# Opening phase of a hybrid block: both modulations on TensorE in four column strips, scaling and splitting of the inputs on VectorE

## The chip, the cores and the metric

The kernel runs on one core of one Trainium2 chip. The metric is the device time of one execution in microseconds (us), the median of the runs shown. A profile is one further execution, recorded by the hardware profiler; its span is the part of that execution that the profile covers.

## The reference

One layer of a block with three token mixers. What the change touches stands at its head: two modulation vectors made from `silu(c)` and `silu(c_ctx)`, and the normalised, modulated inputs on which all projections work.

```python
silu_c, silu_cc = jax.nn.silu(c), jax.nn.silu(c_ctx)
sh1, sc1, g1, sh2, sc2, g2 = jnp.split((silu_c @ w_mod + b_mod)[:, None, :], 6, axis=-1)
csh1, csc1, *_ = jnp.split(silu_cc @ w_mod + b_mod, 6)
h = concatenate([rmsnorm(ctx, norm_mix_w) * (1 + csc1) + csh1,      # 256 tokens
                 rmsnorm(x,   norm_mix_w) * (1 + sc1)  + sh1])      # 512 tokens
out = mixer(h)           # combined input projection, three mixers, gates, output projection
x = x + g1 * out
x = x + g2 * swiglu(rmsnorm(x, norm_ffn_w) * (1 + sc2) + sh2)
result = rmsnorm(x, final_norm_w)
```

The model width is 1024, so `w_mod` is 1024 by 6144. The opening phase needs its first 2048 columns (shift and scale), for both vectors.

## The kernel before

Everything is held with channels on the 128 partitions: x is 8 blocks k of 128 channels by 512 tokens, the context 8 blocks by 256. Projections keep 32-bit accuracy by splitting: each input block becomes a rounded high part H (`hlh`) and a rest L (`hll`), each weight likewise, and `dense` (L313) adds three matmuls per block k (H·H, H·L, L·H), 24 for one output tile ("group") of 128 channels by 512 tokens.

Only TensorE follows an order written out by hand (`MANUAL`, L38 and L1680). The other engines and the DMA queue take their instructions in an order that the tile framework makes from the program. All DMAs are issued from SyncE's queue (SP), which issues in its order and waits where a target buffer is still in use.

`startup` (L1416) is the opening phase. It loads x in four pieces, then the items of `LOADS`, then runs through the words of `STEPS`:

- The modulation of block k for vector s (0 latent, 1 context) is made by `modulate` (L421) on VectorE: two multiply-and-sum instructions (L426) over 128x1024 weights `wmod` against `silu_c`, which holds the vector repeated on all partitions (`silu_c`, made by TensorE at L413), then L429 (bias) and L434 (scale). Blocks 6 and 7 of both vectors are made instead on TensorE by `modulate_pe` (L437): `wmodN`, two more 1 MB loads, as moving operand against the silu columns `scol` (L445), turned by transposes (L451).
- `rstd` (L369) makes the reciprocal root mean square on TensorE, ScalarE and VectorE (L378 to L385); L1470 copies its broadcast to `rbs`.
- `scale_in` (L459) makes H and L of a block. Its form "VV" takes VectorE (L465), ScalarE (L466), VectorE (L467). The other forms put the product (L469) or the difference (L472) on GpSimd and take two ScalarE passes (L470, L471). `EL` and `EX` choose the form of each block.
- Weights come by `fetch` (L209): 256 KB pieces, each in three of `W0` slots, split by ScalarE (L216) and by VectorE and GpSimd in turn (L218). Steps `a` and `b` split the pieces of the first three groups, `g` opens a group on one of the gates.
- A digit runs `dense` for that block on all open groups; six groups are open together, and three more run whole (step `G`). `c` and `C` make the context's `rstd`, `h` its scaled blocks `hx`.

So nine groups of 24 matmuls, 216 in all, run in the opening phase. After it, `first` (L1654) begins with projections of the context: the 48 matmuls that read `hx` into a bank. Then the three mixers follow. Step `D` writes the first three gates out (`gate_out`) and gives their weight slots back, `G` the same for its own.

Of the kernel before, what the change touches and what calls it, by code (L numbers as in the profile page):

```python
# [9 lines left out]
F32 = mybir.dt.float32  # L10
# [9 lines left out]
KT = 8  # L20
# [21 lines left out]
KV = 6  # L42
NK = 3
HO = 6
WB = 4
W0 = 28
NG = 3
GATES = [(b, i) for b in range(3) for i in range(4)]
LOADS = "0 s t 1 2 N"
STEPS = "a m b m l 0 P n m w3 w4 wg n 1 m g wg wg g w5 p 2 g m wu 3 4 n wc 6 c m n 5 C 7 S n n D wg wg G G wg h G"  # L50
EL = "VV VG GV GV GV VG GV VG"
EX = "VV VG VV VG VV VG VV VG"
# [87 lines left out]
class Net:  # L140
# [259 lines left out]
    def silu_c(self, c):  # L400


        sp = self.sp
        t = sp.tile([16, 128], F32, name="silu_r")
        self.S.activation(t, c[:, :128], AF.Tanh, scale=0.5)
        self.V.scalar_tensor_tensor(t, t, 1.0, c[:, :128], op0=OP.add, op1=OP.mult)
        out = sp.tile([128, 2, 1024], F32, name="silu_c")

        def part(s, j):
            b = self.acc_bank()  # L410
            for k in range(4):
                r = 8 * s + 4 * j + k
                self.T.matmul(b[:, 128 * k:128 * k + 128], c[:, 128 + r:129 + r].to_broadcast([16, 128]), t,  # L413
                              start=True, stop=True)
            self.S.copy(out[:, s, 512 * j:512 * j + 512], b)
        return out, part

# [3 lines left out]
    def modulate(self, k, s, silu):  # L421

        V, mod, w = self.V, self.mod, self.wm[k]
        for j in range(2):
            junk = self.sp.tile([128, 1024], BF, name="mjunk", bufs=1)
            V.scalar_tensor_tensor(junk, w[:, j], 0.5, silu[:, s], op0=OP.mult, op1=OP.mult,  # L426
                                   accum_out=mod[:, s, 8 * j + k:8 * j + k + 1])
        z = mod[:, s, k:k + 9:8]
        V.tensor_add(z, z, self.bmod[:, k:k + 9:8])  # L429
        self.scales(k, k + 1, (s,))  # L430

    def scales(self, k0, k1, vectors=(0, 1)):
        for s in vectors:
            self.V.scalar_tensor_tensor(self.sv[:, s, k0:k1], self.mod[:, s, 8 + k0:8 + k1], 1.0,  # L434
                                        self.nmw[:, k0:k1], op0=OP.add, op1=OP.mult)

    def modulate_pe(self, sc, ws):  # L437

        S, V, T, sp = self.S, self.V, self.T, self.sp
        n = KT - KV  # L440
        b, bt = self.bank(), self.bank()
        rows = sp.tile([2, 512], F32, name="silu_r")
        for i, w in enumerate(ws):
            for k in range(KT):
                T.matmul(b[:2, 256 * i:256 * i + 256], sc[:, k], w[:, k], start=(k == 0), stop=(k == KT - 1))  # L445
        S.copy(rows[:, :512], b[:2])
        yield
        for i in range(2):
            for j in range(n):
                o = 2 * (n * i + j)  # L450
                T.transpose(bt[:, o:o + 2], rows[:, 256 * i + 128 * j:256 * i + 128 * j + 128], self.ident[:2, :2])  # L451
        for i in range(2):
            V.tensor_add(self.mod[:, :, 8 * i + KV:8 * i + 8].rearrange("p s j -> p j s"),
                         bt[:, 2 * n * i:2 * n * i + 2 * n].rearrange("p (j s) -> p j s", s=2),
                         self.bmod[:, 8 * i + KV:8 * i + 8].unsqueeze(2).to_broadcast([128, n, 2]))
        self.scales(KV, KT)
        yield

    def scale_in(self, x, n, s, k, H, L, rb, eng):  # L459

        S, V, G = self.S, self.V, self.G
        t = self.sp.tile([128, 512], F32, name="nt", bufs=3)[:, :n]
        scale, shift = self.sv[:, s, k:k + 1], self.mod[:, s, k:k + 1]
        if eng == "VV":
            V.scalar_tensor_tensor(t, x, scale, rb, op0=OP.mult, op1=OP.mult)  # L465
            S.activation(H, t, AF.Identity, bias=shift)  # L466
            V.scalar_tensor_tensor(L, t, shift, H.bitcast(F32), op0=OP.add, op1=OP.subtract)  # L467
        else:
            (G if eng[0] == "G" else V).tensor_mul(t, x, rb)  # L469
            S.activation(H, t, AF.Identity, scale=scale, bias=shift)  # L470
            S.activation(t, t, AF.Identity, scale=scale, bias=shift)  # L471
            (G if eng[1] == "G" else V).tensor_sub(L, t, H.bitcast(F32))  # L472
# [943 lines left out]
    def startup(self):  # L1416
# [3 lines left out]
        c = self.col("crows", [16, 144], pool=sp)  # L1420
        self.wm, wn = {}, []
# [4 lines left out]
        def load(z):  # L1426
            if z.isdigit():
                self.wm[int(z)] = sp.tile([128, 2, 1024], F32, name="wmod", bufs=WB)
                self.dma(self.wm[int(z)], a["wmod1"][int(z)])
            elif z == "N":  # L1430
                for i in range(2):
                    w = sp.tile([128, 2, 1024], F32, name="wmod", bufs=WB).rearrange("p a (b c) -> p (a b) c",
                                                                                      c=128 * (KT - KV))
                    self.dma(w, a["wmodN"][i])
                    wn.append(w)
            elif z == "c":
                self.dma(xc, a["ctxT"])
            elif z in "st":
                for key in first:
                    self.fetch(key, False, ["st".index(z)])  # L1440
            elif z == "g":
                self.fetch(next(fetched), False)
            elif z == "u":
                self.aup0 = self.cp.tile([128, 2, 128], F32, name="TC2")
                self.dma(self.aup0, a["aup"][:, :, :128])
                self.aup0 = self.aup(self.aup0)

        for k in range(0, 8, 2):
            self.dma(x[:, k:k + 2], a["xT"][:, k:k + 2])
            if k == 2:  # L1450
                z = self.col("modc", [128, 88], pool=self.kp)
                self.ident = self.col("ident", [128, 128], pool=self.kp)
        self.bmod, self.nmw, self.nfw, self.fnw = (z[:, i:j] for i, j in ((0, 48), (48, 56), (56, 64), (64, 72)))
        cc = z[:, 72:88].rearrange("p (k s) -> p k s", s=2)
# [3 lines left out]
        silu, part = self.silu_c(c)  # L1458
# [6 lines left out]
        for j in range(2):  # L1465
            part(0, j)
        rb = self.bank()
        self.rstd([sq], TL, 1.0 / D, self.bank(), rb)
        rbs = sp.tile([128, 512], F32, name="rbs")
        S.copy(rbs, rb)  # L1470
# [5 lines left out]
        groups, done, had, had_m, had_n, banks = [], [], [], iter(range(KT)), iter(range(KT)), [3]  # L1476
# [7 lines left out]
        def lat(k):  # L1484
            self.scale_in(x[:, k], TL, 0, k, self.hl[0][k], self.hl[1][k], rbs, EL.split()[k])

        active = iter(gates)
        drained = iter([(0, key) for key in gates])
        for z in STEPS.split():
            if z[0] == "w":  # L1490
                load(z[1:])
            elif z.isdigit():
                k = int(z)
                for n, g in enumerate(groups):
                    ks = [j for j in had + [k] if j not in done[n]] if k not in done[n] else []
                    done[n] += ks
                    self.dense(g, ks=ks)
                had.append(k)
            elif z == "m":
                k = next(had_m)  # L1500
                self.modulate(k, 0, silu)
                lat(k)
            elif z == "n":
                self.modulate(next(had_n), 1, silu)
            elif z == "l":
                part(1, 0)
                part(1, 1)
# [24 lines left out]
            elif z == "P":  # L1532
                sc = sp.tile([128, 8, 2], F32, name="scol")
                S.activation(sc, cc, AF.Tanh, scale=0.5)
                V.scalar_tensor_tensor(sc, sc, 1.0, cc, op0=OP.add, op1=OP.mult)
                V.tensor_scalar(sc, sc, 0.5, None, op0=OP.mult)
                pe = self.modulate_pe(sc, wn)
                next(pe)
            elif z == "p":
                next(pe)  # L1540
                for k in range(KV, KT):
                    lat(k)
            elif z == "c":
                sq = sp.tile([128, 512], F32, name="sq0")[:, :TX]
                for k in range(KT):
                    q = sq if k == 0 else sp.tile([128, 512], F32, name="sqt", bufs=3)[:, :TX]
                    S.activation(q, xc[:, k], AF.Square)
                    if k:
                        (G if k % 2 else V).tensor_add(sq, sq, q)
# [7 lines left out]
            elif z == "h":  # L1557
                for k in range(KT):
                    self.scale_in(xc[:, k], TX, 1, k, self.hx[0][k], self.hx[1][k], rcs, EX.split()[k])
# [405 lines left out]
def lay_out(i):  # L1965
# [10 lines left out]
    A["wmod1"] = f(np.stack([A["wmodT"][:8], A["wmodT"][8:16]], 2))  # L1976
    A["crows"] = f(np.concatenate([A["cvec"].reshape(16, 128), np.eye(16, dtype=np.float32)], 1))
    wm = kp(i["w_mod"][0])
    A["wmodN"] = f(np.stack([wm[:, :, 128 * KV:1024], wm[:, :, 1024 + 128 * KV:2048]], 0))
# [59 lines left out]
```

## Time and profile before

| | us |
|---|---|
| median of 3 runs (1488.23 to 1492.89) | 1488.96 |
| the profiled execution | 1493.02 |
| span of its profile | 1491.2 |
| TensorE busy in the span | 1390.2 |
| last record that reads `hx` in the opening (99.16 + 5.83) | 104.99 |

The profile counts time from the start of the span. "Opening" below means the stretch up to 104.99 us. A true 32-bit matmul is recorded as two instructions; the split ones are recorded as one each. In a row of the timeline, "x2" means that two instructions in a row were merged; the time is from the start of the first to the end of the last, and neighbours overlap, so rates are taken from starts.

### The profile page before, as it was taken

What the parts mean: (1) busy time and instruction counts of PE and PEld (TensorE: products, weight loads), DVE (VectorE), ACT (ScalarE), POOL (GpSimd) and SP (SyncE); (2) the same over time, 40 slices, a digit from 0 to 9 for tenths busy, and PEclk for the clock granted to TensorE, in tenths of its full rate; (3) what the DMA queues carried; (4) which work ended last, traced back from release to release, by engine and by line L of the source; (5) the groups of instructions that cost most, each with busy time, mean ns of one, the idle gap of its engine ahead of it and who ended that gap; (6) DMA issues with size and microseconds to landing.
All of it is one profiled execution on the core that took longest, in us unless ns stands there. A gap on an engine that the chain in (4) does not pass through costs nothing. (4 is left out here: it accounts for less than half of the span.)

```text
span 1491.2 us, 21941 instructions
## 1 busy us (share of the span) xinstructions
PE 1390.2 (93%) x8044; PEld 1194.0 (80%) x8044; DVE 962.1 (65%) x1709; ACT 670.4 (45%) x1254; POOL 393.6 (26%) x345
## 2 busy tenths in 40 slices
PE   5898999999979999998998978999998999999997
PEld 3687879887768887786786867877887999998887
DVE  7957662868494576677675856434438988887332
ACT  4456363553234353333463543333336656566231
POOL 4423522424221212312332706124445000000011
PEclk9999999999999999999999989999999999999998
DMA  7533213142453233236446385656622333324331
GB/s 264 194 107 100 95 56 109 51 124 68 121 148 109 76 93 132 89 101 170 151 154 202 113 261 187 188 176 206 202 78 72 121 107 114 108 91 119 98 91 62
DMA packets 99020, 190.37 MB, mean 128 GB/s; under 512 B 10752, under 2 KB 19472, under 8 KB 97760
## 3 DMA queue, kind: packets, MB, share of 16 engines
q1 hardware_dynamic: 98912, 188.97, 40.8%
q8 instruction: 63, 1.03, 0.3%
q14 instruction: 45, 0.37, 0.1%
HBM read 167.27 MB, written 21.14 MB: 126 GB/s over the span
## 5 line engine op out<-in xcount | busy, mean ns | idle before, releaser
L319 PE MATMUL acc<-hlh,w 128*128 128x512 f32 (+1 forms) x1160 | 388.6, 404 | 6.1 <-ACT w L216 2.0
L216 ACT CAST w<-w 128x512 fp32r<-128x512 f32 (+1 forms) x302 | 182.7, 612 | 377.6 <-DMA w<-in_w_main_dram 172.4
L218 POOL TENSOR_TENSOR w<-w,w 128x512 fp32r<-128x512 f32 x125 | 176.8, 1415 | 541.3 <-ACT w L216 482.4
L218 DVE TENSOR_TENSOR w<-w,w 128x512 fp32r<-128x512 f32 x177 | 136.5, 775 | 210.0 <-ACT w L216 166.5
L319 PEld LDWEIGHTS acc<-hlh,w 128*128 128x128 f32 x1160 | 223.0, 192 | 60.1 <-ACT w L216 2.5
L319 PE MATMUL acc<-hll,w 128*128 128x512 f32 (+1 forms) x576 | 229.4, 398 | 3.7 <-DVE hll L472 1.5
L319 PEld LDWEIGHTS acc<-hll,w 128*128 128x128 f32 x576 | 111.0, 193 | 28.5 <-DVE hll L472 1.9
L319 PE MATMUL acc<-t,w 128*128 128x512 f32 x440 | 115.9, 413 | 7.6 <-ACT t L363 2.9
L319 PEld LDWEIGHTS acc<-t,w 128*128 128x128 f32 x440 | 86.1, 197 | 31.2 <-DVE t L364 4.6
L1809 ACT CAST w<-w 128x512 fp32r<-128x512 f32 x140 | 85.1, 623 | 33.4 <-PE bank L1852 25.7
L1810 DVE TENSOR_TENSOR w<-w,w 128x512 fp32r<-128x512 f32 x140 | 94.9, 688 | 5.0 <-ACT w L1809 4.6
L358 PE MATMUL acc<-w,hlh 128*128 128x256 f32 x512 | 96.9, 289 | 0.1
L1852 PE MATMUL acc<-th,w 128*128 128x256 f32 x480 | 95.3, 281 | 0.2 <-ACT fm L1863 0.2
L1568 POOL TENSOR_TENSOR sq<-sq,sq 128x512 f32<-128x512 f32 x6 | 7.8, 1296 | 307.7 <-ACT sq L1566 307.7
L358 PEld LDWEIGHTS acc<-w,hlh 128*128 128x128 f32 x512 | 81.9, 195 | 3.2 <-issue 1.8
L481 DVE SCALAR_TENSOR_TENSOR cacc<-acc,c_scanc,cacc 128x510 f32<-128x510 f32 (+3 forms) x124 | 77.6, 631 | 5.8 <-ACT cacc L477 5.0
L1852 PEld LDWEIGHTS acc<-th,w 128*128 128x128 f32 x480 | 77.8, 188 | 0.5 <-ACT fm L1863 0.4
L358 PE MATMUL acc<-w,hll 128*128 128x256 f32 x256 | 73.6, 287 | 0.0
L1852 PE MATMUL acc<-tl,w 128*128 128x256 f32 x240 | 67.3, 280 | 0.0
L1411 DVE SCALAR_TENSOR_TENSOR xk<-t 128x1024 bf16<-128x1024 f32 x32 | 42.8, 1337 | 35.6 <-DMA t<-in_wmodT_dram 35.6
L319 PE MATMUL acc<-row,w 128*128 128x512 f32 (+1 forms) x312 | 63.8, 360 | 0.8 <-DVE row L367 0.5
L319 PEld LDWEIGHTS acc<-row,w 128*128 128x128 f32 x312 | 52.1, 188 | 11.2 <-DVE row L367 0.8
(450 smaller groups left out, 2986.6 us busy)
## 6 DMA issues: line engine op xcount, KB each, us to landing
w<-in_w_main_dram SPq DMA_DIRECT2D x180, 256.0 KB, 3.5
w<-in_w_ffs_dram SPq DMA_DIRECT2D x80, 256.0 KB, 2.7
t<-in_wmodT_dram SPq DMA_DIRECT2D x32, 512.0 KB, 4.1
w<-in_w_b_dram SPq DMA_DIRECT2D x48, 256.0 KB, 3.5
xk<-gd SPq DMA_DIRECT2D x40, 256.0 KB, 3.5
w<-in_w_ffo_dram SPq DMA_DIRECT2D x40, 256.0 KB, 2.7
row<-rows SPq DMA_DIRECT2D x16, 512.0 KB, 6.3
wmod<-in_wmod_dram SPq DMA_DIRECT2D x6, 1024.0 KB, 8.6
```

Source lines behind the costliest of these rows:

```text
L216: self.S.copy(h, w)
L218: self.LE[self.wcount % len(self.LE)].tensor_sub(l, w, h.bitcast(F32))
L319: self.T.matmul(dst, w[:, m0:m1], x[:, c0:c1], start=(k == 0 and j == 0), stop=(k == nk - 1 and j == 2))
L358: self.T.matmul(p, x[:, t0:t0 + 128], w, start=(k == 0 and j == 0), stop=(k == KT - 1 and j == 2))
L481: V.scalar_tensor_tensor(acc[:, o0:o1], p[:, o0 + d:o1 + d], w[:, cc, j:j + 1], acc[:, o0:o1], op0=OP.mult, op1=OP.add)
L1411: V.scalar_tensor_tensor(junk, w, 0.5, sc, op0=OP.mult, op1=OP.mult, accum_out=self.mod[:, 0, j:j + 1])
L1568: self.G.tensor_add(a, a, t)
L1809: S.copy(H, x)
L1810: le[p % 7].tensor_sub(L, x, H.bitcast(F32))
L1852: T.matmul(dst, x, y, start=(first and k == 0 and j == 0), stop=(k == 3 and j == 2), skip_group_check=True)
```

## The change

- Order of loads: `modc` (now with a 128x2 matrix of strip sums, `strips`) first, then x, then the modulation weights of block 0, and so on as `LOADS` says. `crows` and `wmodN` are gone. `wmod1` is laid out anew: for each block k one 128x2048 tile, eight chunks of contraction by 256 columns (128 of shift, 128 of scale). Five buffers of it (`WB`), 31 weight slots (`W0`).
- `modulate` becomes one form for all eight blocks and both vectors at once. Eight 32-bit matmuls take the silu columns as stationary operand (128x32, two columns used) and 256 weight columns as moving operand; matmul i+j writes the 32 partitions of strip j of one bank, so that four strips gather two matmuls each. ScalarE copies the bank to `rows`. In a second step two matmuls with `strips` add the four strips and turn rows to columns, and VectorE adds the bias (one instruction) and makes the scale (one).
- `scale_in` always takes the form VectorE, ScalarE, VectorE, for x and for the context. The context's sums of squares are on VectorE alone.
- ScalarE makes one Sqrt early (`rms0`).
- `STEPS` is written anew: `A`k is the first step of a block's modulation, `B`k its second step and `scale_in`, `r` and `R` are the two halves of `rstd`, and a digit may carry `a` (the older half of the open groups) or `b` (the other half).

```diff
-WB = 4
-W0 = 28
+WB = 5
+W0 = 31
-LOADS = "0 s t 1 2 N"
-STEPS = "a m b m l 0 P n m w3 w4 wg n 1 m g wg wg g w5 p 2 g m wu 3 4 n wc 6 c m n 5 C 7 S n n D wg wg G G wg h G"
-EL = "VV VG GV GV GV VG GV VG"
-EX = "VV VG VV VG VV VG VV VG"
+LOADS = "0 s 1 t 2 g 3 g 4"
+STEPS = ("r A0 a w5 R B0 A1 b w6 wg B1 0 A2 w7 1 B2 g A3 1 B3 2 A4 g 2 B4 3 A5 g wg wc 3 B5 4a A6 u 4b B6 5a A7 5b B7 "
+         "6 c 7a C 7b S D wg wg G h G G")
...
-    def modulate(self, k, s, silu):
...
+    def modulate(self, k, w, sc):
+        S, V, T, sp = self.S, self.V, self.T, self.sp
+        b = self.bank()
+        for i in range(0, KT, 4):
+            for j in range(4):
+                T.matmul(b[32 * j:32 * j + 32, :256], sc[:, i + j], w[:, i + j], start=(i == 0), stop=(i == 4))
+        rows = sp.tile([128, 256], F32, name="mrow", bufs=2)
+        S.copy(rows, b[:, :256])
+        yield
         for j in range(2):
...
+            T.matmul(b[:, 256 + 2 * j:258 + 2 * j], rows[:, 128 * j:128 * j + 128], self.strips, start=True, stop=True)
+        V.tensor_add(self.mod[:, :, k:k + 9:8].rearrange("p s j -> p j s"),
+                     b[:, 256:260].rearrange("p (j s) -> p j s", s=2),
+                     self.bmod[:, k:k + 9:8].unsqueeze(2).to_broadcast([128, 2, 2]))
+        V.tensor_scalar(self.sv[:, :, k], self.mod[:, :, 8 + k], 1.0, self.nmw[:, k:k + 1], op0=OP.add, op1=OP.mult)
+        yield
...
-    def scale_in(self, x, n, s, k, H, L, rb, eng):
+    def scale_in(self, x, n, s, k, H, L, rb):
...
-        if eng == "VV":
...
+        V.scalar_tensor_tensor(t, x, scale, rb, op0=OP.mult, op1=OP.mult)
+        S.activation(H, t, AF.Identity, bias=shift)
+        V.scalar_tensor_tensor(L, t, shift, H.bitcast(F32), op0=OP.add, op1=OP.subtract)
...
+        sc = sp.tile([128, 8, 32], F32, name="scol")
+        V.memset(sc, 0.0)
+        t = sp.tile([128, 8, 2], F32, name="scol_t")
+        S.activation(t, cc, AF.Tanh, scale=0.5)
+        V.scalar_tensor_tensor(t, t, 1.0, cc, op0=OP.add, op1=OP.mult)
+        V.tensor_scalar(sc[:, :, :2], t, 0.5, None, op0=OP.mult)
+        S.activation(self.rms0, self.eps, AF.Sqrt)
...
-                        (G if k % 2 else V).tensor_add(sq, sq, q)
+                        V.tensor_add(sq, sq, q)
```

## Rows read from the trace of the kernel before

**Rows 1.** The page, part 1: busy us (share of the span) xinstructions.
```profile
PE 1390.2 (93%) x8044; PEld 1194.0 (80%) x8044; DVE 962.1 (65%) x1709; ACT 670.4 (45%) x1254; POOL 393.6 (26%) x345
```

**Rows 2.** Windows: PE, PEld, DVE, ACT, POOL busy (instructions), granted clock, DMA share, GB/s.
```profile
10.00:15.00 5.00, 2.32 (x10) 2.24 (x11) 3.69 (x7) 2.77 (x5) 0.14 (x1) 1.00 0.93 298
15.00:20.00 5.00, 4.37 (x20) 3.74 (x18) 4.85 (x6) 2.51 (x5) 4.46 (x3) 1.00 1.04 433
...
35.00:40.00 5.00, 5.00 (x13) 1.55 (x14) 4.64 (x9) 2.65 (x4) 2.17 (x1) 0.53 0.33 91
...
70.00:75.00 5.00, 4.20 (x10) 3.12 (x11) 5.00 (x9) 0.26 (x1) 1.06 (x1) 0.54 0.00 0
```

**Rows 3.** Timeline of TensorE in the opening: start, us, what [idle before <-releaser].
```profile
21.30 0.80 PE L319 MATMUL acc<-hlh,w 128*128 128x512 f32 x1 [1.94 <-ACT hlh L466]
...
26.11 3.62 PE L445 MATMUL bank<-wmod,scol 128*2 128x256 f32 x16
35.00 5.91 PE L445 MATMUL bank<-wmod,scol 128*2 128x256 f32 x16 [5.28 <-DMA wmod<-in_wmodN_dram]
...
58.20 0.50 PE L319 MATMUL acc<-hll,w 128*128 128x512 f32 x1 [1.54 <-DVE hll L472]
...
69.37 0.61 PE L378 MATMUL bank<-ones,sq 128*128 128x1 f32 x4 [2.78 <-POOL sq L1549]
...
71.12 0.80 PE L319 MATMUL acc<-hll,w 128*128 128x512 f32 x1 [0.80 <-POOL hll L472]
71.71 1.06 PE L319 MATMUL acc<-hlh,w 128*128 128x512 f32 x2
...
72.99 1.05 PE L319 MATMUL acc<-hlh,w 128*128 128x512 f32 x2
...
95.42 0.62 PE L319 MATMUL bank<-hlh,w 128*128 128x512 f32 x2
...
96.12 0.63 PE L319 MATMUL bank<-hlh,w 128*128 128x512 f32 x2
...
99.16 5.83 PE L319 MATMUL bank<-hx,w 128*128 128x256 f32 x48
```

**Rows 4.** Waits of the DMA queue (SP) in the opening: total us, times, longest.
```profile
SPq L224 <- POOL w L218: 16.7, 2, 15.9
SPq L1434 <- DVE mod L429: 15.5, 1, 15.5
```

**Rows 5.** Groups of instructions up to 130 us: busy us, mean ns, idle before.
```profile
L426 DVE SCALAR_TENSOR_TENSOR mjunk<-wmod,silu_c 128x1024 bf16<-128x1024 f32 x24 | 31.4, 1306 | 1.2 <-DMA wmod<-in_wmod_dram 1.1
```

**Rows 6.** Timeline of all engines, from the first modulation to the first `dense`.
```profile
11.97 1.22 DVE L426 SCALAR_TENSOR_TENSOR mjunk<-wmod,silu_c 128x1024 bf16<-128x1024 f32 x1
...
12.11 1.87 PE L378 MATMUL bank<-ones,sq 128*128 128x1 f32 x8 [5.28 <-DVE sq L1464]
...
14.54 1.11 PE L385 MATMUL bank<-c_ident,rcol 128*128 128x128 f32 x4 [0.57 <-DVE rcol L382]
...
19.74 0.75 DVE L465 SCALAR_TENSOR_TENSOR nt<-x,sv,rbs 128x512 f32<-128x512 f32 x1
...
20.53 0.72 ACT L466 ACTIVATE hlh<-nt,mod 128x512 fp32r<-128x512 f32 x1 [2.25 <-DVE nt L465]
...
21.61 0.75 DVE L467 SCALAR_TENSOR_TENSOR hll<-nt,mod,hlh 128x512 fp32r<-128x512 f32 x1
...
28.83 0.15 DVE L434 SCALAR_TENSOR_TENSOR sv<-mod,c_modc 128x1 f32<-128x1 f32 x1
```

**Rows 7.** Timeline of TensorE later: 32-bit matmuls into one half, then into both.
```profile
343.30 1.93 PE L795 MATMUL bank<-xk,t 128*64 128x512 f32 x4
...
358.22 1.24 PE L358 MATMUL acc<-w,hx 128*128 128x256 f32 x9
359.39 1.08 PE L808 MATMUL bank<-xk,t 128*64 128x512 f32 x4
360.40 0.50 PE L358 MATMUL acc<-w,hlh 128*128 128x256 f32 x2
```

More of the change, by code (lines that the diff above doesn't have):

```diff
@@ L41 @@
 AHEAD = 4
-KV = 6
 NK = 3
 HO = 6
-WB = 4
-W0 = 28
+WB = 5
+W0 = 31
 NG = 3
 GATES = [(b, i) for b in range(3) for i in range(4)]
-LOADS = "0 s t 1 2 N"
-STEPS = "a m b m l 0 P n m w3 w4 wg n 1 m g wg wg g w5 p 2 g m wu 3 4 n wc 6 c m n 5 C 7 S n n D wg wg G G wg h G"
-EL = "VV VG GV GV GV VG GV VG"
-EX = "VV VG VV VG VV VG VV VG"
+LOADS = "0 s 1 t 2 g 3 g 4"
+STEPS = ("r A0 a w5 R B0 A1 b w6 wg B1 0 A2 w7 1 B2 g A3 1 B3 2 A4 g 2 B4 3 A5 g wg wc 3 B5 4a A6 u 4b B6 5a A7 5b B7 "
+         "6 c 7a C 7b S D wg wg G h G G")
 W3 = 23
@@ L398, in setup @@
         self.rms0 = self.kp.tile([128, 1], F32, name="rms0")
[L400 to L416, printed above, removed]
@@ L418, in modbias @@
     def modbias(self, s, j0, j1):
         self.V.tensor_add(self.mod[:, s, j0:j1], self.mod[:, s, j0:j1], self.bmod[:, j0:j1])
-    def modulate(self, k, s, silu):
-        V, mod, w = self.V, self.mod, self.wm[k]
-        for j in range(2):
[L425 to L446, printed above, removed]
-        yield
[L448 to L457, printed above, removed]
@@ L459, in scale_in @@
-    def scale_in(self, x, n, s, k, H, L, rb, eng):
-        S, V, G = self.S, self.V, self.G
+    def modulate(self, k, w, sc):
[7 more added lines that the diff above has]
+        yield
+        for j in range(2):
+            T.matmul(b[:, 256 + 2 * j:258 + 2 * j], rows[:, 128 * j:128 * j + 128], self.strips, start=True, stop=True)
[3 more added lines that the diff above has]
+        V.tensor_scalar(self.sv[:, :, k], self.mod[:, :, 8 + k], 1.0, self.nmw[:, k:k + 1], op0=OP.add, op1=OP.mult)
+        yield
@@ L462, in scale_in @@
+    def scale_in(self, x, n, s, k, H, L, rb):
+        S, V = self.S, self.V
         t = self.sp.tile([128, 512], F32, name="nt", bufs=3)[:, :n]
         scale, shift = self.sv[:, s, k:k + 1], self.mod[:, s, k:k + 1]
-        if eng == "VV":
[L465 to L472, printed above, removed]
+        V.scalar_tensor_tensor(t, x, scale, rb, op0=OP.mult, op1=OP.mult)
+        S.activation(H, t, AF.Identity, bias=shift)
+        V.scalar_tensor_tensor(L, t, shift, H.bitcast(F32), op0=OP.add, op1=OP.subtract)
@@ L1419, in startup @@
         x, xc = sp.tile([128, 8, 512], F32, name="x0"), sp.tile([128, 8, 256], F32, name="xc0")
-        c = self.col("crows", [16, 144], pool=sp)
-        self.wm, wn = {}, []
+        wm, mods = {}, {}
         first = [("small",), ("gqk", 0, 0), ("gqk", 0, 1)]
@@ L1427, in load @@
             if z.isdigit():
[L1428 to L1435, printed above, removed]
+                wm[int(z)] = sp.tile([128, 2048], F32, name="wmod", bufs=WB).rearrange("p (k c) -> p k c", c=256)
+                self.dma(wm[int(z)], a["wmod1"][int(z)])
             elif z == "c":
@@ L1442, in load @@
                 self.fetch(next(fetched), False)
[L1443 to L1446, printed above, removed]
+        z = self.col("modc", [128, 90], pool=self.kp)
         for k in range(0, 8, 2):
             self.dma(x[:, k:k + 2], a["xT"][:, k:k + 2])
[L1450 to L1454, printed above, removed]
+        self.ident = self.col("ident", [128, 128], pool=self.kp)
+        self.bmod, self.nmw, self.nfw, self.fnw, cc, self.strips = (
+            z[:, i:j] for i, j in ((0, 48), (48, 56), (56, 64), (64, 72), (72, 88), (88, 90)))
+        cc = cc.rearrange("p (k s) -> p k s", s=2)
         for z in LOADS.split():
             load(z)
-        silu, part = self.silu_c(c)
+        sc = sp.tile([128, 8, 32], F32, name="scol")
[5 more added lines that the diff above has]
+        S.activation(self.rms0, self.eps, AF.Sqrt)
         sq = sp.tile([128, 512], F32, name="sq0")
@@ L1464, in startup @@
                 V.tensor_add(sq, sq, q)
-        for j in range(2):
-            part(0, j)
+        rbs = sp.tile([128, 512], F32, name="rbs")
         rb = self.bank()
-        self.rstd([sq], TL, 1.0 / D, self.bank(), rb)
-        rbs = sp.tile([128, 512], F32, name="rbs")
-        S.copy(rbs, rb)
+        rx = self.rstd_gen([sq], TL, 1.0 / D, self.bank(), rb)
         for j in range(4):
@@ L1475, in startup @@
                     self.hx[z].append(t[:, 512 * i + 256 * z:512 * i + 256 * z + 256])
-        groups, done, had, had_m, had_n, banks = [], [], [], iter(range(KT)), iter(range(KT)), [3]
+        groups, done, banks = [], [], [3]
         def group(key):
@@ L1484, in lat @@
         def lat(k):
-            self.scale_in(x[:, k], TL, 0, k, self.hl[0][k], self.hl[1][k], rbs, EL.split()[k])
+            self.scale_in(x[:, k], TL, 0, k, self.hl[0][k], self.hl[1][k], rbs)
         active = iter(gates)
-        drained = iter([(0, key) for key in gates])
         for z in STEPS.split():
@@ L1491, in startup @@
                 load(z[1:])
[L1492 to L1501, printed above, removed]
-                lat(k)
[L1503 to L1507, printed above, removed]
+            elif z[0] == "A":
+                k = int(z[1])
+                mods[k] = self.modulate(k, wm[k], sc)
+                next(mods[k])
+            elif z == "r":
+                next(rx)
+            elif z == "R":
+                next(rx, None)
+                S.copy(rbs, rb)
+            elif z[0] == "B":
+                k = int(z[1])
+                next(mods[k])
+                lat(k)
+            elif z[0].isdigit():
+                k, n = int(z[0]), len(groups) // 2
+                for i in dict(a=range(n), b=range(n, len(groups))).get(z[1:], range(len(groups))):
+                    ks = [j for j in range(k + 1) if j not in done[i]]
+                    done[i] += ks
+                    if ks:
+                        self.dense(groups[i], ks=ks)
+            elif z == "u":
+                self.aup0 = self.cp.tile([128, 2, 128], F32, name="TC2")
+                self.dma(self.aup0, a["aup"][:, :, :128])
+                self.aup0 = self.aup(self.aup0)
             elif z == "a":
@@ L1531, in startup @@
                 self.release(key)
[L1532 to L1542, printed above, removed]
             elif z == "c":
@@ L1558, in startup @@
                 for k in range(KT):
-                    self.scale_in(xc[:, k], TX, 1, k, self.hx[0][k], self.hx[1][k], rcs, EX.split()[k])
+                    self.scale_in(xc[:, k], TX, 1, k, self.hx[0][k], self.hx[1][k], rcs)
+        assert all(sorted(z) == list(range(KT)) for z in done)
         self.groups = [g[0] for g in groups[:3]]
@@ L1975, in lay_out @@
     A["wmodT"] = f(i["w_mod"][0].T.reshape(48, 128, 1024))
-    A["wmod1"] = f(np.stack([A["wmodT"][:8], A["wmodT"][8:16]], 2))
-    A["crows"] = f(np.concatenate([A["cvec"].reshape(16, 128), np.eye(16, dtype=np.float32)], 1))
     wm = kp(i["w_mod"][0])
-    A["wmodN"] = f(np.stack([wm[:, :, 128 * KV:1024], wm[:, :, 1024 + 128 * KV:2048]], 0))
+    A["wmod1"] = f(np.stack([np.concatenate([wm[:, :, c + 128 * k:c + 128 * k + 128] for c in (0, 1024)], 2)
+                             for k in range(8)], 0))
     A["modc"] = f(np.concatenate([cols(z) for z in (i["b_mod"][0], i["norm_mix_w"][0], i["norm_ffn_w"][0],
                                                     i["final_norm_w"])] +
-                                 [A["cvec"].reshape(2, 8, 128).transpose(2, 1, 0).reshape(128, 16)], 1))
+                                 [A["cvec"].reshape(2, 8, 128).transpose(2, 1, 0).reshape(128, 16),
+                                  (np.arange(128)[:, None] % 32 == np.arange(2)).astype(np.float32)], 1))
     main = []
```

## The prediction

> **What bounds the kernel now.** I read the page first: TensorE is busy for 1390.2 of 1491.2 us [rows 1], so the kernel as a whole ends when TensorE has done its list, and a change can only matter where TensorE idles, runs at its lower clock, or does work that can go. The opening (up to 104.99 us) is such a place. Its own matmuls are few: nine groups of 24 plus the context's 48. At the higher clock three matmuls of 512 columns take 96.12 - 95.42 = 0.70 us, 0.233 us each [rows 3], so 216 take 50.3 us, and the context's 48 take 5.8 [rows 3]. That is 56 us of 105.
>
> I then followed TensorE's timeline [rows 3] and account for the rest so: 21.3 us before the first `dense`; 9.5 us for blocks 6 and 7 of the modulation (3.62 + 5.91) and some 1.4 for their transposes and the context's `rstd`; waits of 5.28 (weights `wmodN`), 1.54, 2.78 and 0.80, together 10.4 us; and the lower clock. In 35 to 40 and 70 to 75 us the granted clock is 0.53 and 0.54 [rows 2], that is 1.2 GHz, each time after TensorE had idled; in the second of these three matmuls take 72.99 - 71.71 = 1.28 us, 0.43 each [rows 3]. The first nine matmuls (21.30 to 26.11) go at that pace too. Against 0.233 each this costs 2.7 us at the start and some 3.2 after 71 us, 5.9 in all. The sum, 21.3 + 50.3 + 5.8 + 9.5 + 1.4 + 10.4 + 5.9 = 104.6, meets the 104.99 of the trace.
>
> Who made TensorE wait? VectorE. It is busy for 3.7 to 5.0 us of every 5 [rows 2]; 24 multiply-and-sums of 1.31 us, 31.4 us, are the modulation [rows 5]. It is late with blocks (1.54), and the load of the second `wmodN` stands 15.5 us in the DMA queue for a buffer that VectorE still reads [rows 4], from which the wait of 5.28 follows. The other two waits end with GpSimd.
>
> **The change part by part.** All sums are against the profiled execution (1493.02 us, span 1491.2, so 1.8 lie outside); it stands 4.1 us above the median of 1488.96, and I take the same number of us off the median.
>
> *Modulation on TensorE (A).* One block costs eight 32-bit matmuls of 256 columns, 16 records. Before, 16 such records in a row take 3.62 us, a step of (3.62 - 0.38) / 15 = 0.216 with the last one's 0.38 taken off [rows 3]. Unshared, A would be 3.5 us, twice that at 1.2 GHz. Whether strips run side by side is the question of this change, and the trace has a near case: four 32-bit records into one half of a bank take 1.93 us, but four of the same shape into two halves 1.08 [rows 7]. Two strips take the time of one. No row has four. The bounds are 2 side by side (A = 1.73 us) and 4 (0.86). I take 4, as the two halves lost nothing to each other, and add 0.25 us for going in and out of strips: the nine matmuls before the two-strip block go at 0.12, so it starts about 0.1 late, and the next begins 0.15 after its second 0.43 us step would have ended [rows 7]. A is 1.1 us at the higher clock and 2.0 at the lower.
>
> The Trainium skill, "TensorE: Matmul & The Clock Gate", section "Measured speedup vs the span model", gives 2.38 times for three column strips, less than in proportion, which speaks against my 4. The trace's two halves show no such loss. By that page four strips would give an estimated 3.2 times and A 1.3 us, and the sum below would be 1.3 us longer.
>
> *Second step (B).* Two 32-bit matmuls with two columns, four records: the nearest rows are the one-column records of the ones-matmul, four in 0.61 us [rows 3] and, at the start and the lower clock, eight in 1.87 [rows 6]; I take 0.6, and 0.9 for B0. ScalarE's copy to `rows` is half as wide as the 0.72 us pass of L466 [rows 6] and lies under a digit's matmuls for A2 to A7.
>
> *VectorE.* It loses the 31.4 us and the small ones behind them. Per latent block it now has two small instructions (0.15 each [rows 6]) and two passes of 0.75 [rows 6], 1.8 us, for eight blocks 14.4, against 5.6 us of `dense` per block over nine groups. H and L of a block are ready some 3 us after B (0.3 + 0.75 + 0.72 + 0.75 and hops), and from block 2 on each B stands 3 us or more of matmuls ahead of its first use. So the pass that GpSimd did costs TensorE nothing; if that cover were gone, it would be the chain's 2.5 us a block. The context's eight blocks lie under three whole groups (17 us), and its sums of squares under digit 6. The waits of 1.54, 2.78 and 0.80 go with their cause; what is late next is at most a block whose VectorE pass collides with a weight split, for which I keep 1 us.
>
> *Loads.* Ahead of block 0's weights go 3.25 MB with them (x, `modc`, `ident`), ahead of blocks 1, 2, 3, 4 in all 5.1, 6.9, 8.5 and 10.1 MB, then some 11.1, 12.2 and (behind a gate) 13.8 for 5, 6 and 7. The queue moved 298 and 433 GB/s in two busy windows [rows 2]. At their mean of 366, from 2 us on, block 0 is there at 11.1 (in the row of before it is read at 11.97 [rows 6]), then 16, 21, 25, 30, 33, 35 and 40. TensorE wants them (19 us, the start below, plus the digits, A and B ahead of each) at about 12, 15.5, 23, 28, 33, 40, 46 and 52. Only block 1 is late, by under 1 us. At 298 the later ones come at 25, 31, 36, 39, 43 and 48, which makes three of them 2 to 3 us late in turn, 3 us in all: that is the other end. In the queue `w5`, `w6`, a gate and `w7` wait for A0, for A1, for the splits of step `b`, for A2, and stand before all later loads. The longest such wait in the trace is 15.9 us for a split on GpSimd [rows 4]; were it to strike there, `w7` would land near 50, still not after its use. The new order and the two more slots I cost at nothing on this ground.
>
> *Start.* In before the ones-matmul of `rstd` starts at 12.11, after ScalarE's squares, among which two copies of `silu_c` stood; without them I put it at 11. From there: 1.9 (rstd) [rows 6], A0 2.0, transposes 1.1 [rows 6], B0 0.9, VectorE and ScalarE 0.3 + 0.75 + 0.72 [rows 6], hops about 0.6; A1 and B1 lie beside this. The first `dense` starts near 19 instead of 21.30. The early Sqrt only moves a table load that was hidden.
>
> *The sum from there.* 50.3 (216 matmuls) + 1.8 (first nine at the lower clock) + 6 x 1.1 (A2 to A7) + 6 x 0.6 (B2 to B7) + 1.0 (context's `rstd`) + 5.8 (context) + 1.0 (small waits) = 70.1 us. From 19, the opening ends at 89 instead of 105, **16 us** sooner. By parts: start 2.3; L445 and its transposes 9.9 for A and B 10.2; waits 9.4; clock 4.1, since TensorE no longer idles between its first group and the end.
>
> *What follows.* The weights of the next stage wait in the queue for slots that the last gates and the small projection give back, before and after; VectorE and GpSimd are not behind at that point. So the rest should move as one piece, and the kernel end 16 us sooner: 1488.96 - 16 = 1473.
>
> **The rivals.**
>
> *Two at a time.* Four strips go no faster than two. A becomes 2.0 (5.4 us more over six blocks), A0 and A1 1.7 more each at the lower clock, of which A1 hides part behind its load: some 8 us, so 1481. For it: only two are shown [rows 7].
>
> *One after another.* If 32-wide strips don't overlap at all (the change then doesn't do what it says), A is 3.5 + 0.25: 2.6 x 6 = 15.6 us more, and A0 and A1, 6.9 each at the lower clock and both ahead of the first `dense`, put it 9.7 us later, less 1.8 as the clock is up by then. 23.5 us: 1496.5, slower. The change stops paying from an A of about 3 us. Against it: the halves [rows 7].
>
> *Starved.* The loads come at 298 GB/s or one sits behind a wait in the queue, or VectorE's passes stretch beside GpSimd's splits and a block is late more than once; TensorE then idles and drops its clock as it did at 35 and 71 us, for 5 to 8 us: 1478 to 1481.
>
> *Given back.* The opening ends sooner but what follows it (constants and weights loaded late, gates on ScalarE and VectorE) doesn't: up to the whole 16 us, 1480 to 1489. Against it: those loads are released by TensorE's own progress.
>
> **How the numbers follow.** Forecast 0.64; two at a time 0.11; starved 0.12; given back 0.08, half of it within 0.3% of before (about what can be told from no change, 4.5 us); one after another 0.05. The likeliest alone: start 18 to 20.5, A 0.9 to 1.3, waits 0 to 3, so 1469 to 1477. To hold 8 in 10 I reach to the two-strip and starved cases above, 1483, and below to 1467 (waits none, strips without switching cost, first `dense` at 17.5). Faster 0.87 (all of forecast, two at a time and starved, half of given back, minus a little for what I haven't seen), same 0.06, slower 0.07.
>
> **What would show it.** Right: the last `hx` matmul of the opening ends at 86 to 92 us; 16 records of a block's A span 1.0 to 1.4 us; the granted clock stays at 2.4 GHz from about 25 us on; no wait over 2 us on TensorE between the first `dense` and the context; VectorE near half busy there. Wrong: A of 1.7 or more, a stretch near 0.5 of clock after 25 us, `dense` waiting for `wmod` or for `hll`, or a gap after the opening that is longer than before's.

## The result, and the profile after

The changed kernel takes 1478.51 us (median of 20 runs, 1470.6 to 1485.47) against 1489.7 for the kernel before (20 runs, 1482.61 to 1499.98): a ratio of 0.9916, 95% interval 0.9901 to 0.9931, or 12.5 us (10.3 to 14.8); the two medians themselves lie 11.2 apart. A second timing beside the kernel before gave 0.9932 (0.9911 to 0.9954; medians 10.2 apart). The forecast was 1473, with a range of 1467 to 1483.

The profiled execution took 1470.6 us with a span of 1468.6. It was the fastest of the 20, so its span must not be set against before's; its opening can be. The timeline of TensorE in the opening of the changed kernel (start, us, what, idle before):

```profile
11.91 1.87 PE L376 MATMUL bank<-ones,sq 128*128 128x1 f32 x8 [11.91 <-DVE sq L1414]
13.71 1.93 PE L408 MATMUL bank<-wmod,scol 128*32 128x256 f32 x16
15.57 1.11 PE L383 MATMUL bank<-c_ident,rcol 128*128 128x128 f32 x4
16.48 0.84 PE L413 MATMUL bank<-c_modc,mrow 128*128 128x2 f32 x4
17.66 1.07 PE L408 MATMUL bank<-wmod,scol 128*32 128x256 f32 x16 [0.34 <-DMA wmod<-in_wmod_dram]
20.41 0.89 PE L413 MATMUL bank<-c_modc,mrow 128*128 128x2 f32 x4 [1.68 <-ACT mrow L410]
21.16 0.77 PE L317 MATMUL acc<-hlh,w 128*128 128x512 f32 x1
...
24.40 0.40 PE L317 MATMUL acc<-hlh,w 128*128 128x512 f32 x1
24.73 1.07 PE L408 MATMUL bank<-wmod,scol 128*32 128x256 f32 x16
25.73 0.51 PE L317 MATMUL acc<-hlh,w 128*128 128x512 f32 x1
...
27.93 0.50 PE L413 MATMUL bank<-c_modc,mrow 128*128 128x2 f32 x4
28.36 1.07 PE L408 MATMUL bank<-wmod,scol 128*32 128x256 f32 x16
...
83.34 5.90 PE L317 MATMUL bank<-hx,w 128*128 128x256 f32 x48
91.28 0.57 PE L482 MATMUL bank<-c_ident,row 48*128 48x48 f32 x6 [2.04 <-ACT row L1612]
```

The opening ends at 83.34 + 5.90 = 89.24 us, where the last row of [rows 3] gives 104.99. L408 is A, L413 is B. An A takes 25.73 - 24.73 = 1.00 us until the next matmul starts. From the first `dense` at 21.16 to the end of the opening there is no wait of a microsecond left.

The windows of 20 to 66 us (busy us and instructions of PE, PEld, DVE, ACT, POOL, granted clock, DMA share, GB/s), first of the kernel before in a second profile, then of the changed one:

```profile
20.00:66.00 46.00, 37.73 (x135) 23.84 (x136) 43.56 (x72) 19.30 (x35) 21.51 (x13) 0.93 0.63 229
```

```profile
20.00:66.00 46.00, 45.35 (x271) 33.62 (x272) 25.38 (x50) 19.60 (x42) 9.22 (x7) 0.96 0.60 230
```

VectorE falls from 43.6 to 25.4 of 46 us, TensorE rises from 37.7 to 45.4, and the DMA moves the same. The engine that set the pace is no longer VectorE.

### The profile page after: what moved, and what is told of

Same layout as the page of the kernel before. It is cut to its first block, busy times and chain, and to the rows that moved or that the text cites. A ratio compares the mean times of both kernels' runs of the same rounds, so it can differ in the third digit from the quotient of the medians.

```text
span 1468.6 us, 22065 instructions
## 1 busy us (share of the span) xinstructions
PE 1375.5 (94%) x8136; PEld 1186.9 (81%) x8136; DVE 931.8 (63%) x1664; ACT 664.3 (45%) x1247; POOL 368.4 (25%) x330
## 3 DMA queue, kind: packets, MB, share of 16 engines
q8 instruction: 64, 1.05, 0.3%
## 5 line engine op out<-in xcount | busy, mean ns | idle before, releaser
L317 PE MATMUL acc<-hlh,w 128*128 128x512 f32 (+1 forms) x1160 | 384.4, 400 | 3.4 <-ACT hlh L1529 1.5
L216 POOL TENSOR_TENSOR w<-w,w 128x512 fp32r<-128x512 f32 x125 | 172.8, 1383 | 566.0 <-ACT w L214 503.4
L317 PE MATMUL acc<-hll,w 128*128 128x512 f32 (+1 forms) x576 | 226.4, 393 | 0.9 <-POOL hll L1531 0.9
L317 PE MATMUL acc<-t,w 128*128 128x512 f32 x440 | 112.2, 404 | 5.4 <-DVE t L362 2.5
L436 DVE SCALAR_TENSOR_TENSOR cacc<-acc,c_scanc,cacc 128x510 f32<-128x510 f32 (+3 forms) x124 | 77.6, 631 | 6.8 <-ACT cacc L432 6.0
```

The lines of the kernel that those rows point to most:

```text
L216: self.LE[self.wcount % len(self.LE)].tensor_sub(l, w, h.bitcast(F32))
L317: self.T.matmul(dst, w[:, m0:m1], x[:, c0:c1], start=(k == 0 and j == 0), stop=(k == nk - 1 and j == 2))
L436: V.scalar_tensor_tensor(acc[:, o0:o1], p[:, o0 + d:o1 + d], w[:, cc, j:j + 1], acc[:, o0:o1], op0=OP.mult, op1=OP.add)
```

## The experiments

The table gives, for each profile, the start of the first `dense`, the end of the opening's last `hx` matmul, and the rest of the span.

| kernel | first `dense` | opening ends | rest of the span |
|---|---|---|---|
| before | 21.30 | 104.99 | 1386.2 |
| before, second profile | 21.61 | 104.06 | 1388.9 |
| changed | 21.16 | 89.24 | 1379.4 |
| changed, second profile | 21.20 | 89.40 | 1383.0 |
| changed, third profile | 21.17 | 90.29 | 1387.7 |
| one strip | 25.55 | 108.79 | 1389.3 |
| two strips | 22.98 | 95.95 | 1384.1 |
| GpSimd shares the splitting | 22.31 | 91.07 | 1389.8 |
| four buffers | 21.23 | 90.67 | 1388.0 |
| before, VectorE alone | 20.69 | 100.46 | 1383.8 |
| second block early | 22.55 | 92.82 | 1388.3 |
| first digit ahead of B1 | 20.24 | 90.15 | 1383.2 |

**One strip and two.** The question is whether strips side by side carry the gain.

```diff
-        for i in range(0, KT, 4):
-            for j in range(4):
-                T.matmul(b[32 * j:32 * j + 32, :256], ..., start=(i == 0), stop=(i == 4))
+        for i in range(0, KT, N):          # N = 1 or 2; rows, strips cut to 32 * N partitions
+            for j in range(N):
+                T.matmul(b[32 * j:32 * j + 32, :256], ..., start=(i == 0), stop=(i == KT - N))
```

> The changed kernel with all eight modulation matmuls of a block in one strip, so that none can run beside another. Theory (the opening is bound by TensorE's list, and strips side by side make the modulation cheap): a block's 16 records take 3.5 to 3.9 us at 2.4 GHz instead of 1.07, six blocks 15 to 17 us more after the first dense matmul, and the two before it at the lower clock 8 to 10 us more; the opening ends at 110 to 116 us instead of 89.2, and the kernel is as slow as before or up to 10 us slower. Rival (the gain comes from freeing VectorE, and TensorE has room): the opening ends within 5 us of 89.2.

> The changed kernel with two strips of four matmuls each. Theory: a block's 16 records take 1.9 to 2.1 us at 2.4 GHz, six blocks 5.2 to 6 us more and the start 2 to 3.5 later; the opening ends at 95 to 99 us, and the kernel is 6 to 10 us slower than the changed one. Rival (TensorE has room): the opening ends within 2 us of 89.2.

The timeline of TensorE with one strip, then with two:

```profile
27.84 3.64 PE L408 MATMUL bank<-wmod,scol 128*32 128x256 f32 x16
...
102.89 5.90 PE L317 MATMUL bank<-hx,w 128*128 128x256 f32 x48
```

```profile
25.26 1.92 PE L408 MATMUL bank<-wmod,scol 128*32 128x256 f32 x16
...
90.05 5.90 PE L317 MATMUL bank<-hx,w 128*128 128x256 f32 x48
```

The same 16 records take 3.64, 1.92 and 1.07 us with one, two and four strips. The three times fit one rule: 0.2 us common to all (fitted, not measured by itself), and 3.44, 1.72 and 0.87 besides. Two strips halve that part and four quarter it. The opening ends at 108.8 and 96.0 instead of 89 to 90, and the kernels come to 1497.82 (ratio to before 1.0047, 1.0029 to 1.0064) and 1485.79 us (0.9959, 0.9935 to 0.9984). The theory holds, and so does the slower rival's price: with one strip the change would have lost. Only the start was less costly than expected with one strip (25.55, not 29 or more), so the end lies just below the 110 to 116 given: TensorE runs without a wait from 11.81 to 24.5 us, and its clock is up before the first A ends, which takes 6.27 us instead of 6.9; the transposes behind it take 0.65 instead of 1.11.

**GpSimd back in the changed kernel.** `scale_in` with its two forms, `EL`, `EX` and the shared sums of the kernel before.

```diff
-    def scale_in(self, x, n, s, k, H, L, rb):
+    def scale_in(self, x, n, s, k, H, L, rb, eng):      # body, EL and EX as before the change
...
-                        V.tensor_add(sq, sq, q)
+                        (G if k % 2 else V).tensor_add(sq, sq, q)
```

> The changed kernel with the scaling and splitting of the inputs and the context's sums shared out between VectorE and GpSimd as before the change. Theory (the modulation on TensorE carries the gain, the pass on GpSimd lies under dense matmuls): the opening ends at 89 to 93 us; early blocks may be late by up to 2.5 us once or twice. Rival (VectorE alone for scaling and splitting is what brings the gain): the opening ends at 97 us or later.

The opening ends at 91.07, 0.8 to 1.8 us later than in the changed kernel's three profiles. The loss is at the start: the first `dense` comes 1.1 later (22.31), and from there to the end it takes 68.8 us, where the changed kernel's profiles take 68.1 to 69.1. Timeline of GpSimd and VectorE, then the same VectorE instruction in the changed kernel:

```profile
18.03 1.27 POOL L432 TENSOR_TENSOR nt<-x,rbs 128x512 f32<-128x512 f32 x1
18.20 1.65 DVE L428 SCALAR_TENSOR_TENSOR nt<-x,sv,rbs 128x512 f32<-128x512 f32 x1
```

```profile
18.07 0.75 DVE L425 SCALAR_TENSOR_TENSOR nt<-x,sv,rbs 128x512 f32<-128x512 f32 x1
```

VectorE's pass over the first block lasts 1.65 us beside GpSimd's product for a later one, and 0.75 without it; ScalarE makes H 1.0 later. So in the changed kernel the VectorE form is worth about 1 us, by one profile. The timing, 0.9893 (0.9846 to 0.994, four runs), can't tell this kernel from the changed one.

**VectorE alone in the kernel before.** The same part of the change, made in the other kernel.

```diff
-EL = "VV VG GV GV GV VG GV VG"
-EX = "VV VG VV VG VV VG VV VG"
+EL = "VV VV VV VV VV VV VV VV"
+EX = "VV VV VV VV VV VV VV VV"
...
-                        (G if k % 2 else V).tensor_add(sq, sq, q)
+                        V.tensor_add(sq, sq, q)
```

> The kernel before with one part of the change alone: VectorE scales and splits all inputs and adds the context's squares. Theory (VectorE bounds the opening of before, by the modulation it makes): its list grows by some 6 us of passes for x and 4 for the context; the opening ends at 105 to 111 us instead of 104.99, no faster. Rival (GpSimd's slow passes of 1.8 us and the stretched VectorE instructions beside them are what makes the blocks late): the opening ends at 102 us or sooner.

My theory fell. The opening ends at 100.46, 3.6 to 4.5 us sooner, and the kernel takes 1484.1 us (ratio 0.9961, 0.9941 to 0.998). Groups of VectorE's instructions up to 105 us (busy us, mean ns | idle before), first of the kernel before, then with VectorE alone:

```profile
L426 DVE SCALAR_TENSOR_TENSOR mjunk<-wmod,silu_c 128x1024 bf16<-128x1024 f32 x24 | 31.4, 1307 | 1.4 <-DMA wmod<-in_wmod_dram 1.3
L434 DVE SCALAR_TENSOR_TENSOR sv<-mod,c_modc 128x1 f32<-128x1 f32 (+1 forms) x14 | 7.9, 572 | 0.1
L429 DVE TENSOR_TENSOR mod<-mod,c_modc 128x2 f32<-128x2 f32 x12 | 5.0, 417 | 0.2
```

```profile
L426 DVE SCALAR_TENSOR_TENSOR mjunk<-wmod,silu_c 128x1024 bf16<-128x1024 f32 x24 | 29.4, 1223 | 0.9 <-DMA wmod<-in_wmod_dram 0.9
L434 DVE SCALAR_TENSOR_TENSOR sv<-mod,c_modc 128x1 f32<-128x1 f32 (+1 forms) x14 | 5.3, 391 | 0.0
L429 DVE TENSOR_TENSOR mod<-mod,c_modc 128x2 f32<-128x2 f32 x12 | 3.0, 247 | 0.1
```

The kernel before is shown by its second profile. These three groups alone take 6.6 us less, though nothing in them changed. What stretched them stands in the timeline of the kernel before, and behind it the same VectorE instruction with GpSimd's product gone:

```profile
18.67 1.25 POOL L469 TENSOR_TENSOR nt<-x,rbs 128x512 f32<-128x512 f32 x1
18.76 1.18 DVE L434 SCALAR_TENSOR_TENSOR sv<-mod,c_modc 128x1 f32<-128x1 f32 x1
```

```profile
18.86 0.16 DVE L434 SCALAR_TENSOR_TENSOR sv<-mod,c_modc 128x1 f32<-128x1 f32 x1
```

A VectorE instruction on one column lasts 1.18 us and ends at 19.94, when GpSimd's ends at 19.92; alone it takes 0.16. So what VectorE took over cost it no more than GpSimd had taken from it: it is busy for 77.7 of 105 us before and 77.6 after. The Trainium skill, "SBUF — State Buffer", section "Who interferes with whom", says that a VectorE instruction with two inputs in SBUF contends with a GpSimd instruction that reads there. The trace agrees, by the 1.18 and 0.16 us.

GpSimd also stood in TensorE's way itself: the waits of 2.78 and 0.80 us that it ended in [rows 3] are gone, and the waits at one block have grown, from 0.34 and 1.54 us in the second profile of before to 3.08 and 0.73:

```profile
56.62 0.80 PE L319 MATMUL acc<-hlh,w 128*128 128x512 f32 x1 [3.08 <-ACT hlh L466]
```

The edit takes away GpSimd's late results and its contention together; how the 4 us divide between the two isn't shown. Nor do the two parts of the change add up: alone, this one brings some 4 us of opening and the rest of the change 13.5 (91.07 in the kernel above), together they bring 14.9.

**Four buffers.**

```diff
-WB = 5
+WB = 4
```

> The changed kernel with four buffers of modulation weights instead of five. Theory (the loads run ahead of their use from the third block on): the opening ends within 1 us of 89.2. Rival (the fifth buffer keeps the DMA queue from standing): the weights of blocks 4 to 7 land late, TensorE waits for wmod, and the opening ends 3 us or more later.

The opening ends at 90.67, outside the 1 us that I gave, but TensorE waits for no `wmod` in it. It stays at the lower clock a little longer instead. Timeline, then windows of this kernel (columns as above):

```profile
24.79 0.63 PE L317 MATMUL acc<-hlh,w 128*128 128x512 f32 x1
25.35 1.90 PE L408 MATMUL bank<-wmod,scol 128*32 128x256 f32 x16
```

```profile
20.00:25.00 5.00, 4.64 (x13) 3.67 (x13) 3.70 (x7) 2.57 (x6) 1.95 (x2) 0.53 1.01 396
25.00:30.00 5.00, 5.00 (x34) 2.97 (x37) 0.78 (x2) 0.89 (x2) 0.66 (x1) 0.79 1.03 425
```

The clock rises after 25 us here, and A2 takes 1.90 us; in the changed kernel's first profile it rises before 25 (granted 0.66 in 20 to 25 us) and A2 takes 1.07. Its third profile, with five buffers, ends as late, at 90.29: A2 takes 1.55 us, and only 13 matmuls pass in 20 to 25 us as here, though the column of the granted clock reads 1.00. At the start the pace of the matmuls is the better witness. The fifth buffer gives nothing that these profiles can tell.

**Two tries at the start.** In the changed kernel H of the first block is made by ScalarE from 18.86 to 19.58 us, yet the first `dense` starts at 21.16: B1 stands ahead of it in TensorE's order and waits for ScalarE's copy. Timeline of ScalarE:

```profile
18.86 0.72 ACT L426 ACTIVATE hlh<-nt,mod 128x512 fp32r<-128x512 f32 x1 [1.55 <-DVE nt L425]
19.49 0.60 ACT L214 CAST w<-w 128x512 fp32r<-128x512 f32 x1
20.00 0.36 ACT L410 COPY mrow<-bank 128x256 f32<-128x256 f32 x1
```

One try loads the second block earlier and puts A1 right behind A0; the other only exchanges B1 and the first digit.

```diff
-LOADS = "0 s 1 t 2 g 3 g 4"
-STEPS = ("r A0 a w5 R B0 A1 b w6 wg B1 0 A2 ...
+LOADS = "0 1 s t 2 g 3 g 4"                          # first try
+STEPS = ("r A0 a w5 A1 R B0 B1 b w6 wg 0 A2 ...      # first try
+STEPS = ("r A0 a w5 R B0 A1 b w6 wg 0 B1 A2 ...      # second try, LOADS as in the changed kernel
```

> The changed kernel with the second block's modulation weights loaded ahead of the first block's projection weights, its first step put right behind the first one's, and the first digit put behind B1. Theory (in the changed kernel TensorE stood 1.7 us for ScalarE's copy ahead of B1, with the first block's H ready at 19.6 us): the first dense matmul starts at 19.5 to 20.5 us instead of 21.16 and the opening ends at 87.5 to 88.7. Rival (the later weights of the first groups, or ScalarE's order, now hold the first digit): it ends at 89 us or later.

> The changed kernel with one exchange in TensorE's order: the first digit ahead of B1 instead of behind it, loads as in the changed kernel. Theory (the 1.7 us for ScalarE's copy stand in TensorE's way at 18.7 us, and the second block's H and L, 3 us behind B1, then stand in the way of the second digit): the first dense matmul starts at 19.6 to 20.2 us instead of 21.16, some 0.5 to 1.5 us of that return as a wait before the second digit, and the opening ends at 88 to 89.5. Rival (the second digit waits for the whole gain or more): the first dense matmul starts at 19.6 to 20.2 all the same, and the opening ends at 89.5 or later.

The first try is worse: A1 at the lower clock pushes R and B0 back by 1.4 us (B0 at 17.84 instead of 16.48), and VectorE then makes the scales of both blocks ahead of its first pass over x, which starts at 21.00 instead of 18.07. The first `dense` starts at 22.55, and the opening ends at 92.82 (1482.18 us, ratio 0.9942, 0.992 to 0.9963). The second starts at 20.24 and pays it back before the second digit:

```profile
23.53 0.50 PE L413 MATMUL bank<-c_modc,mrow 128*128 128x2 f32 x4
23.96 1.07 PE L408 MATMUL bank<-wmod,scol 128*32 128x256 f32 x16
26.09 0.49 PE L317 MATMUL acc<-hlh,w 128*128 128x512 f32 x1 [1.06 <-ACT hlh L426]
26.88 0.50 PE L317 MATMUL acc<-hll,w 128*128 128x512 f32 x1 [0.29 <-DVE hll L427]
```

It ends at 90.15, no sooner than the changed kernel, as the rival said. But its `rstd` began late (12.52, against 11.80 to 11.91 in the changed kernel's profiles), so half a microsecond of gain isn't excluded. None of these versions is shown to beat the changed one. The new order of loads and the three more weight slots were not run by themselves.

**Once more, both.** Is the opening's gain the kernel's gain?

> The kernel before, once more, for its profile. If the opening is fixed and only what follows it varies from execution to execution, its opening ends within 0.5 us of 104.99, and what follows takes 1380 to 1390 us (1386.2 in the first profile).

> The changed kernel, once more, for its profile. The opening ends within 1 us of 89.2, and what follows takes 1384 to 1390 us, as in the variants, where the first profile has 1379.4: the first profile was a lucky execution. Rival (what follows is really shorter by 7 us in the changed kernel): 1377 to 1382 us again.

> The changed kernel once more, timed in five rounds beside the kernel before. Theory (the gain is that of the opening, 14.7 to 15.8 us by its profiles, and what follows is alike): a ratio of 0.989 to 0.991, and in its profile an opening of 89 to 90.5 us and 1380 to 1390 us behind it. Rival (some 3 us are given back behind the opening): a ratio of 0.9915 to 0.993.

The openings repeat: 104.06 and 104.99 against 89.24, 89.40 and 90.29, a gain of 14.9 us between the means. (The first of before lies 0.9 from the other, not 0.5.) The rest of the span goes from 1379.4 to 1389.8 us: its mean is 1386.3 for the three profiles with before's order of steps, and 1385.6 for the changed kernel's three and the four variants that end the opening before 93 us (1385.9 with one strip and two). The second profile's 1383.0 lies between the ranges of theory and rival, and the mean of the changed kernel's own three is 1383.4; with a spread of 10 us that is no difference. The first profile was a lucky execution, and its 1468.6 is no measure of the change. The third profile's timing, 0.9932, lies outside the theory's 0.989 to 0.991 and just above the rival's 0.9915 to 0.993.

## Why the prediction was right or wrong

**What bounded the opening** was read rightly: TensorE waited, for VectorE's modulation. That GpSimd's instructions were part of why VectorE was late I didn't see, though the stretched groups stood in the trace, and two of the four waits, as I noted myself, ended with GpSimd's own results. I costed the VectorE form at nothing for TensorE, and it is worth about 1 us in the changed kernel and some 4 in the kernel before.

**The strips** were right: 1.00 us per A from start to next start, 1.1 in the sum. Four strips lose nothing to each other (3.44 to 0.87), as the two halves of [rows 7] did not; the Trainium skill's figure for three column strips ("TensorE: Matmul & The Clock Gate", section "Measured speedup vs the span model"), weighed there, would have had A at 1.3. The cost of going in and out, 0.25 in the sum, is 24.73 - 24.40 - 0.233 = 0.1 on the way in and, with the fitted 0.87, 25.73 - 24.73 - 0.87 = 0.13 on the way out.

**The start** was the mis-sized step: 19 forecast, 21.16 measured. I put the ones-matmul at 11 on the ground that the copies of `silu_c` were in ScalarE's way; without them it starts at 11.91, since ScalarE waits for the second half of x and its last four squares begin at 8.12 us. And I let A1 and B1 lie beside the chain, where B1 stands in front of the first `dense` and waits 1.68 us. The early Sqrt doesn't do what I said either: ScalarE loads a table for it, then one for Tanh, then one for Sqrt again, as this timeline shows; all three lie hidden.

```profile
0.73 1.28 ACT L1408 ACT_TABLE_LOAD   x1 [0.73 <-PEq L1974]
...
2.25 1.28 ACT L1405 ACT_TABLE_LOAD   x1
...
8.12 2.44 ACT L1412 ACTIVATE sqt<-x 128x512 f32<-128x512 f32 x4 [0.84 <-DMA x<-in_xT_dram]
...
10.57 1.28 ACT L379 ACT_TABLE_LOAD   x1
```

**The sum from the first `dense`** was 70.1 us and is 89.24 - 21.16 = 68.1. B was too dear (0.43 us from 27.93 to 28.36, against 0.6), A a little, and of the 1 us kept for waits 0.24 came; the first matmul behind an A takes 0.1 longer than its 0.233 (25.73 to 26.07), which gives some of it back. So the end of the opening, 89, was right because a start 2 us too early met a walk 2 us too long.

**Waits and clock** went where the sum said: no wait on `wmod` after the first 0.34 us, none on `hll`, and the granted clock stays full from 25 us to the end of the opening. That is the first profile; by its matmuls the third gets there about 1 us later, and ends 1.05 later.

**What follows** was the step that cost the rest. The opening gives 14.9 us; the timed kernel 12.5 (10.3 to 14.8) and 10.1 (6.9 to 13.3) in the second timing. I had it move as one piece. Part of the difference is seen: TensorE's first wait behind the opening is 2.04 to 2.16 us in the changed kernel's three profiles, where it is 1.32 and 1.24 in before's, because three splits of ScalarE stand ahead of the copy that it waits for, and two in before. Timeline of ScalarE, changed kernel first:

```profile
88.64 1.72 ACT L214 CAST w<-w 128x512 fp32r<-128x512 f32 x3 [0.73 <-POOL w L216]
90.38 0.58 ACT L1611 COPY row<-acc 48x512 f32<-48x512 f32 x1
90.86 0.36 ACT L1612 COPY row<-bank 48x256 f32<-48x256 f32 x1
```

```profile
104.25 1.14 ACT L216 CAST w<-w 128x512 fp32r<-128x512 f32 x2 [0.86 <-DMA w<-in_w_main_dram]
105.41 0.58 ACT L1667 COPY row<-acc 48x512 f32<-48x512 f32 x1
105.89 0.36 ACT L1668 COPY row<-bank 48x256 f32<-48x256 f32 x1
```

That is 0.7 to 0.9 us. With it the gain is some 14.1, inside the first interval and above the second's upper end. The variants suggest that more is given back. The table sets each opening (against 104.5, the mean of before's two) beside the distance of the timed medians; variants that ran once are left out:

| kernel | opening, us | timed, us | given back |
|---|---|---|---|
| changed (mean opening; two timings) | -14.9 | -11.2, -10.2 | 3.7, 4.7 |
| GpSimd shares the splitting | -13.5 | -10.7 | 2.7 |
| second block early | -11.7 | -6.7 | 5.0 |
| two strips | -8.6 | -5.4 | 3.1 |
| one strip | +4.3 | +6.6 | 2.3 |
| before, VectorE alone | -4.1 | -4.8 | -0.7 |

Taken singly most of these differences are within the noise, and every opening but the first is from one profile. But each kernel with the changed order loses 2 to 5 us of its opening again, and the one with before's order doesn't. (By the ratios instead of the medians the four runs of the second row, at -16.0, fall out of line; the others give back 2.4 to 4.8.) Where it goes beyond the first 0.7 to 0.9 us stays open: the rest of the span varies by 10 us between profiles, and twelve can't tell it.

## What to carry to other kernels

A matrix-vector product whose weights stream through TensorE as moving operand can be cut along its contraction into four 32-wide column strips of one bank, which small matmuls then add: here the 16 records went from 3.64 to 1.07 us, for 0.36 to 0.47 us of adding at the higher clock. Without the strips this change would have lost. Where VectorE is late, look for short VectorE instructions that last as long as a GpSimd instruction beside them: taking work from GpSimd can then free VectorE. And read a change in one stage from that stage's end in several profiles; one execution's span may be off by more than half the gain.

## What the runs showed of the hardware

At the entry to the feed-forward part TensorE waits 1.5 to 2.5 us for ScalarE, and then the clock either stays up or falls. The two profiles of the kernel before have the same instructions and the same wait there, and part behind it. Each first line is the wait, each second one a window (columns as above), first profile, then second:

```profile
1125.08 0.38 PE L319 MATMUL acc<-hlh,w 128*128 128x256 f32 x1 [1.48 <-ACT hlh L1585]
1130.00:1135.00 5.00, 4.82 (x41) 4.61 (x41) 5.00 (x10) 2.65 (x8) 1.30 (x2) 1.00 0.25 73
```

```profile
1124.31 0.38 PE L319 MATMUL acc<-hlh,w 128*128 128x256 f32 x1 [1.48 <-ACT hlh L1585]
1130.00:1135.00 5.00, 5.00 (x28) 5.00 (x29) 3.24 (x6) 1.29 (x4) 0.82 (x1) 0.60 0.21 52
```

At full clock 41 matmuls pass in 5 us; with a mean of 0.60, most of it at 1.2 GHz, 28. From the 24 matmuls on `row` ahead of the wait to TensorE's next wait of over 4 us it takes 35.4 us in the first profile and 38.2 in the second. Over all twelve profiles it is 35.4 twice (before and changed, the first profile of each), 36.1 once and 38.2 to 39.9 in nine, so this one place makes 3 to 4.5 us of the spread between executions.
